# A hybrid decoder layer on one core: the emitter's estimate also books the splits of the weights

## The chip, the cores and the metric

The kernel runs on one core of a Trainium2 chip. The metric is the device time of one execution in microseconds (us), lower is better.

## The reference

One decoder layer over 2048 tokens of width 1024, all in float32. Both branches read the same normed input through one combined projection.

```python
h = rms_norm(x, attn_norm)
proj = h @ w_in                       # gated delta-net q/k/v, z, beta, a; attention q/k/v; two gates
dn_qkv, dn_z, dn_b, dn_a, sq, sk, sv, gate_raw = split_combined(proj)
y_dn  = gated_deltanet_branch(dn_qkv, dn_z, dn_b, dn_a, ...)   # 4 heads of 128, conv of 4, chunks
y_swa = sliding_window_branch(sq, sk, sv, ...)                 # 8 heads of 64, window 128, bias, sinks
gates = sigmoid(gate_raw)
merged = gates[0] * (y_dn @ w_branch_dn) + gates[1] * (y_swa @ w_branch_swa)
x = x + merged @ w_out
h2 = rms_norm(x, ffn_norm)
x = x + (silu(h2 @ w_gate) * (h2 @ w_up)) @ w_down             # inner width 2816
```

## The kernel before

The 2048 tokens are worked in four blocks of 512 (0 to 3). The large matrix products of a block are the dense work. Each float32 operand is split in a high and a low part in a format that TensorE multiplies in one pass, and a product is three matmuls: high by high, high by low, low by high (`mm3`, `tok_mm`). The weights come in 120 units, 118 of 128 by 1024 and two of 128 by 1056 (`skv`). A unit of 1024 serves 24 matmuls of 512 columns, and one dense step is three matmuls.

A unit is fetched by `weights` (lines 154 to 183), which is called right ahead of the unit's first matmul. In block 0 it loads the raw unit (`wraw`, 2 buffers), and for each half ACT copies the high part (line 168) and DVE or POOL subtracts for the low part (line 171; both halves on POOL for the first three units, then the first half on DVE and the second on POOL). Both parts lie in one tile `whl` (5 buffers). Each half is also stored in DRAM. Blocks 1 to 3 load the stored halves straight into `whl` (line 181) and split nothing.

The dense work of a block runs in this order: `skv` and `sq` (keys, values and queries of the attention), the mixer (per delta-net head three `dn` units, one `z` unit; 16 gate units; 4 units of the attention branch; 4 units of the delta-net merge), `wo`, then the feed-forward part in five pieces of `up` and `down`. Block b+1's `skv` and `sq` stand between `wo` and `up` of block b.

All else on TensorE comes from side programs (`norm1`, `norm2`, `skv_post`, `swa`, `dn_post`, two lanes of `dn_cores`, and others): generators that hand out a few instructions on TensorE, DVE, ACT and POOL and then yield until those are done. TensorE's order is fixed by the order of emission (`manual_schedule`), the other engines' order is made by the scheduler, with a higher priority for side programs.

Where a side step goes is settled by `Estimate`. `note` (lines 72 to 94) books each instruction that is emitted through the wrapper `Noted`: it starts when TensorE's own estimated clock `now`, the engine's `free` time and the `ready` times of its inputs plus HOP (220 ns) have passed, and takes a time that grows with its columns. A TensorE instruction moves `now` to its end. What an instruction writes becomes `ready` at its end, by the name of the tile. A side is due when what its step gave out is done, plus HOP and SLACK (30 ns), line 241. `drive` (208 to 228) emits a side step as soon as one is due by `now` and a PSUM bank is free by the estimate, and a dense step otherwise. When dense work waits for a side, sides are emitted until it can go on. `weights` alone takes the unwrapped object, `self.raw`, so that its ACT, DVE and POOL instructions are not booked. Loads are never booked (line 105).

Of the kernel before, what the change touches and what calls it, by code (L numbers as in the profile page):

```python
# [114 lines left out]
class Emitter:  # L115
# [36 lines left out]


    def weights(self, key, a):
        nc = self.raw
        n = a * 264 if key[0] == "skv" else 1024
        h = a // 2
        hl = []
        if key not in self.kept:
            src = self.w_skv[key[1]] if key[0] == "skv" else self.w_all[UNITS[key]]  # L160
            raw = self.wp.tile([P, 1056], F32, name="wraw", tag="wraw", bufs=WR)
            nc.sync.dma_start(out=raw[:, :n], in_=src)
            keep = []
            for j in range(2):
                t = self.wp.tile([P, 2, 528], F32R, name="whl", tag="whl", bufs=WB)
                r = raw[:, j * n // 2:(j + 1) * n // 2]
                hi, lo = t[:, 0, :n // 2], t[:, 1, :n // 2]
                nc.scalar.activation(hi, r, AF.Copy)  # L168
                self.nsub += 1
                eng = nc.vector if self.nsub > 6 and self.nsub % PSUB else nc.gpsimd  # L170
                eng.tensor_tensor(out=lo, in0=r, in1=hi, op=ALU.subtract)  # L171
                if self.nblocks > 1:
                    d = self.kp.tile([P, 2, n // 2], F32, name="wk", tag="wk%d_%d" % (len(self.kept), j))
                    nc.sync.dma_start(out=d, in_=t[:, :, :n // 2].bitcast(F32))
                    keep.append(d)
                hl.append([t[:, e, :n // 2].rearrange("p (a m) -> p a m", a=h) for e in range(2)])
            self.kept[key] = keep
        else:
            for j in range(2):
                t = self.wp.tile([P, 2, 528], F32R, name="whl", tag="whl", bufs=WB)  # L180
                nc.sync.dma_start(out=t[:, :, :n // 2].bitcast(F32), in_=self.kept[key][j])
                hl.append([t[:, e, :n // 2].rearrange("p (a m) -> p a m", a=h) for e in range(2)])
        return lambda k: (hl[k // h][0][:, k % h], hl[k // h][1][:, k % h])
# [914 lines left out]
```

## Time and profile before

| | |
|---|---|
| median of 3 runs | 3195.55 us (3194.09 to 3197.91) |
| profiled execution | 3196.13 us, span 3194.3 us |
| PE (matmul) busy | 3095.3 us, 97% |
| PEld (weight load) busy | 2523.6 us, 79% |
| DVE busy | 1403.2 us, 44% |
| ACT busy | 837.6 us, 26% |
| POOL busy | 415.8 us, 13% |
| mean granted TensorE clock | 0.990 |
| moved by DMA | 595.99 MB |

All times come from one profiled execution. A line of the view in order of time merges neighbouring instructions of one kind: start, length, engine, source line, operation, what it writes and reads, count, and in brackets how long the engine sat idle before it and what ended that. Nearly all instructions carry line 109, that of the wrapper, so they are told apart by the names of their tiles: `kn` and `qr` are normed keys and queries of the attention, `xn` the normed input of the feed-forward part, `R` and `W` belong to the triangular solve of a delta-net head, `O` is a head's output.

### The profile page before, as it was taken

Reading aid. Unit: us, or ns where it says so; the run is one execution under the profiler, and the core shown is the slowest. Engines: PE = TensorE matmul, PEld = TensorE weight load, DVE = VectorE, ACT = ScalarE, POOL = GpSimd, SP = SyncE. Lnnn points to the kernel's source line nnn. Section 1 sums busy time; section 2 is a strip of 40 time slices with the busy share of each in tenths; the row PEclk is TensorE's granted clock in tenths of the full one; section 3 lists DMA queues with packets and bytes.
Section 4 is the critical chain, followed back from the end, with each engine's and each line's share of the span. In section 5 each row is a group of like instructions: output and inputs, shape, how many; then the busy total and the mean of one; then the engine's idle time right before and its main releaser. Section 6 shows DMA issues by size and latency. Waiting matters only on the chain. (4 is left out here: it accounts for less than half of the span.)

```text
span 3194.3 us, 39761 instructions
## 1 busy us (share of the span) xinstructions
PE 3095.3 (97%) x14854; PEld 2523.6 (79%) x14854; DVE 1403.2 (44%) x3626; ACT 837.6 (26%) x2112; POOL 415.8 (13%) x401
## 2 busy tenths in 40 slices
PE   7888989999999999999999999999999999999999
PEld 5776778778888887878887888877888888878887
DVE  5867656533336544542215565443221655422221
ACT  4454334422323322330002323232000233110000
POOL 2433211322212100010001110011000211000000
PEclk9999999999999999999999999999999999999999
DMA  6554475588874446445556445545566544645565
GB/s 240 185 178 152 154 251 209 198 284 285 283 254 145 132 142 215 153 152 191 184 192 200 131 143 179 177 154 170 190 189 205 169 131 133 198 159 193 192 189 183
DMA packets 291848, 595.99 MB, mean 187 GB/s; under 512 B 18975, under 2 KB 20168, under 8 KB 291656
## 3 DMA queue, kind: packets, MB, share of 16 engines
q1 hardware_dynamic: 277648, 569.20, 54.1%
q10 hardware_dynamic: 14008, 24.25, 2.2%
q8 instruction: 117, 1.92, 0.2%
q14 instruction: 75, 0.61, 0.1%
HBM read 459.08 MB, written 134.30 MB: 186 GB/s over the span
## 5 line engine op out<-in xcount | busy, mean ns | idle before, releaser
L109 PE MATMUL acc<-h,whl 128*128 128x512 f32 x7296 | 1760.1, 397 | 7.5 <-DVE whl L171 4.9
L109 PEld LDWEIGHTS acc<-h,whl 128*128 128x128 f32 x7296 | 1357.6, 189 | 313.9 <-DVE whl L171 5.8
L109 PE MATMUL acc<-whl,a 128*128 128x512 f32 x2112 | 493.7, 393 | 0.0
L109 PEld LDWEIGHTS acc<-whl,a 128*128 128x128 f32 x2112 | 395.5, 188 | 90.3
L109 DVE TENSOR_TENSOR x<-x,acc 128x512 f32<-128x512 f32 x192 | 131.4, 687 | 390.4 <-PE acc L109 388.6
L171 POOL TENSOR_TENSOR whl<-wraw,whl 128x512 fp32r<-128x512 f32 (+1 forms) x123 | 167.0, 1359 | 565.4 <-ACT whl L168 472.6
L168 ACT ACTIVATE whl<-wraw 128x512 fp32r<-128x512 f32 (+1 forms) x240 | 149.0, 630 | 290.3 <-PE acc L109 136.1
L109 DVE TENSOR_TENSOR th<-th,acc 128x512 f32<-128x512 f32 x88 | 60.4, 687 | 316.0 <-PE acc L109 315.8
L109 DVE SCALAR_TENSOR_TENSOR th<-th,acc 128x512 f32<-128x512 f32 x88 | 60.5, 687 | 304.9 <-ACT th L109 304.9
L109 PE MATMUL acc<-whl,mt 128*128 128x512 f32 x768 | 181.9, 398 | 8.1 <-DVE h L109 7.6
L109 ACT ACTIVATE th<-acc 128x512 f32<-128x512 f32 x88 | 52.7, 598 | 499.5 <-PE acc L109 499.3
L109 PEld LDWEIGHTS acc<-whl,mt 128*128 128x128 f32 x768 | 145.9, 191 | 43.2 <-DVE h L109 8.5
L109 DVE SCALAR_TENSOR_TENSOR cv<-xr,cst_sb,cv 128x512 f32<-128x512 f32 x144 | 134.6, 935 | 60.7 <-ACT cv L109 53.1
L109 ACT ACTIVATE a<-th 128x512 fp32r<-128x512 f32 x88 | 55.5, 631 | 346.8 <-DVE th L109 332.1
L171 DVE TENSOR_TENSOR whl<-wraw,whl 128x512 fp32r<-128x512 f32 x117 | 89.8, 768 | 121.4 <-ACT whl L168 120.9
L109 PE MATMUL acc<-whl,h 128*128 128x264 f32 (+1 forms) x768 | 139.8, 341 | 0.0
L109 PEld LDWEIGHTS acc<-whl,h 128*128 128x128 f32 x768 | 118.0, 188 | 16.7 <-issue 1.1
L109 POOL COPY ccar<-xr 128x3 f32<-128x3 f32 x48 | 9.0, 188 | 858.5 <-ACT xr L109 858.5
L109 PE MATMUL acc<-sp,whl 128*128 128x512 f32 x384 | 103.2, 409 | 0.0
L109 POOL TENSOR_TENSOR pT<-pT,cst_sb 128x512 f32<-128x512 f32 x62 | 82.7, 1362 | 137.2 <-ACT pT L109 121.1
L109 ACT ACTIVATE L<-L,ast 128x256 f32<-128x256 f32 (+1 forms) x192 | 83.4, 457 | 60.0 <-DVE ast L109 60.0
L109 PE MATMUL acc<-ydn,whl 128*128 128x512 f32 x384 | 92.6, 401 | 0.4
(183 smaller groups left out, 2817.5 us busy)
## 6 DMA issues: line engine op xcount, KB each, us to landing
whl<-wk SPq DMA_DIRECT2D x708, 512.0 KB, 3.9
wk<-whl SPq DMA_DIRECT2D x236, 512.0 KB, 3.5
wraw<-in_w_all SPq DMA_DIRECT2D x118, 512.0 KB, 5.0
x<-in_x ACTq DMA_DIRECT2D x56, 256.0 KB, 5.1
out<-x ACTq DMA_DIRECT2D x32, 256.0 KB, 3.8
whl<-wk SPq DMA_DIRECT2D x12, 528.0 KB, 5.1
wk<-whl SPq DMA_DIRECT2D x4, 528.0 KB, 2.7
x<-in_x SPq DMA_DIRECT2D x8, 256.0 KB, 6.5
```

Of the source, the lines that this page charges most:

```text
L109: r = f(*args, **kw)
L168: nc.scalar.activation(hi, r, AF.Copy)
L171: eng.tensor_tensor(out=lo, in0=r, in1=hi, op=ALU.subtract)
```

## The change

The function `weights` takes the wrapped object. Its ACT copies and its DVE and POOL subtractions are then booked by `Estimate.note` like every other instruction, in their place in the emission; its DMAs are handed on as before. The instructions themselves stay the same.

```diff
     def weights(self, key, a):
-        nc = self.raw
+        nc = self.nc
         n = a * 264 if key[0] == "skv" else 1024
         h = a // 2
         hl = []
```

## Rows read from the trace of the kernel before

**Rows 1.** The page's engine totals: busy us, share of the span, instructions.

```profile
PE 3095.3 (97%) x14854; PEld 2523.6 (79%) x14854; DVE 1403.2 (44%) x3626; ACT 837.6 (26%) x2112; POOL 415.8 (13%) x401
```

**Rows 2.** Busy by stretch: us, PE, PEld, DVE, ACT, POOL, granted clock, DMA share, GB/s.

```profile
100.00:200.00 100.00, 88.73 (x412) 70.54 (x410) 82.79 (x222) 44.41 (x122) 46.78 (x40) 0.95 0.50 174
...
69.00:320.00 251.00, 223.19 (x1120) 178.90 (x1119) 185.52 (x504) 118.43 (x340) 92.64 (x84) 0.95 0.51 176
320.00:412.00 92.00, 79.27 (x437) 65.69 (x436) 56.67 (x145) 33.17 (x79) 20.74 (x15) 0.93 0.52 178
412.00:487.00 75.00, 72.41 (x322) 58.50 (x321) 39.78 (x71) 29.17 (x62) 14.36 (x10) 0.98 0.69 241
487.00:528.00 41.00, 40.06 (x241) 34.95 (x240) 23.86 (x86) 16.19 (x40) 1.28 (x1) 1.00 0.54 190
528.00:645.00 117.00, 111.49 (x526) 86.11 (x525) 70.06 (x209) 58.21 (x157) 44.07 (x37) 0.99 0.60 206
645.00:927.00 282.00, 282.00 (x1221) 228.90 (x1220) 89.55 (x131) 80.34 (x131) 63.63 (x49) 1.00 0.82 285
927.00:3195.00 2268.00, 2240.57 (x10754) 1832.50 (x10752) 900.75 (x2348) 471.62 (x1240) 164.37 (x185) 1.00 0.53 172
```

**Rows 3.** The tile whl, its splits: count, ns min/median/max, first and last start.

```profile
L168 ACT ACTIVATE whl<-wraw x240: 612/632/690, 13.1 to 915.6; 128x512 fp32r<-128x512 f32 x118, 128x528 fp32r<-128x528 f32 x2
L171 POOL TENSOR_TENSOR whl<-wraw,whl x123: 1262/1301/2055, 13.8 to 916.3; 128x512 fp32r<-128x512 f32 x119, 128x528 fp32r<-128x528 f32 x4
L171 DVE TENSOR_TENSOR whl<-wraw,whl x117: 673/692/1778, 34.9 to 913.8; 128x512 fp32r<-128x512 f32 x117
```

**Rows 4.** PE's waits over the span: us in total, times, longest.

```profile
PE acc L109 <- DVE whl L171: 4.9, 2, 3.1
```

**Rows 5.** PE in order of time: first steps of side programs, and dense work.

```profile
51.36 1.30 PE L109 MATMUL aux<-cst_sb,kn 128*128 128x128 f32 x8 [0.77 <-DVE kn L109]
...
430.02 2.19 PE L109 MATMUL aux<-cst_sb,x 128*128 128x128 f32 x12
...
502.81 2.34 PE L109 MATMUL aux<-cst_sb,xn 128*128 128x128 f32 x20
...
527.97 14.04 PE L109 MATMUL acc<-h,whl 128*128 128x512 f32 x60
541.85 0.60 PE L109 MATMUL aux<-cst_sb,qr 128*128 128x128 f32 x4
```

**Rows 6.** ACT and DVE in order of time: the chains ahead of those steps.

```profile
40.93 0.18 ACT L109 ACTIVATE ba<-acc 128x8 f32<-128x8 f32 x1 [0.55 <-PE acc L109]
...
429.28 3.26 DVE L109 TENSOR_SCALAR x<-x,st 128x512 f32<-128x512 f32 x8
...
487.83 0.69 DVE L109 TENSOR_TENSOR x<-x,acc 128x512 f32<-128x512 f32 x1 [0.69 <-PE acc L109]
491.89 3.26 DVE L109 TENSOR_SCALAR xn<-x,st 128x512 f32<-128x512 f32 x8
499.55 0.18 ACT L109 ACTIVATE ba<-acc 128x8 f32<-128x8 f32 x1 [0.38 <-PE acc L109]
503.86 1.42 DVE L109 TENSOR_TENSOR kn<-kr,kst 128x256 f32<-128x256 f32 x4
535.05 2.50 DVE L109 TENSOR_TENSOR qr<-qr,qst 128x512 f32<-128x512 f32 x4
```

**Rows 7.** PE's matmuls on weights (tile whl) in one stretch: us, busy, clock, DMA.

```profile
69.00:320.00 251.00, 166.36 (x658) 0.95 0.51 176
```

**Rows 8.** ACT and PE in order of time, around two waits of PE.

```profile
361.92 0.63 ACT L168 ACTIVATE whl<-wraw 128x512 fp32r<-128x512 f32 x1 [5.13 <-DMA wraw<-in_w_all]
362.46 0.58 ACT L109 ACTIVATE W<-aux 128x512 f32<-128x512 f32 x1
363.09 2.08 PE L109 MATMUL aux<-R,W 128*128 128x128 f32 x8 [4.32 <-ACT W L109]
...
411.65 1.12 PE L109 MATMUL aux<-cst_sb,O 128*128 128x128 f32 x4 [5.77 <-DVE O L109]
```

## The prediction

> **What bounds the kernel now.** I read the engine totals first: PE is busy 97% of the span [rows 1]. With so full an engine the question is where the other 99 us lie, so next came the busy time by stage [rows 2]. The reader is to see three things in it. From 927 us on (blocks 1 to 3) PE is busy 2240.57 of 2268 us, so all three leave 27 us idle. From 645 to 927 us PE is busy 282 of 282, at the full clock, although this stretch splits weights all the time and has no side steps. The rest is in block 0: from 69 to 645 us PE idles 27.8 + 12.7 + 2.6 + 0.9 + 5.5 = 49.5 us, and in four of these five stretches the granted clock is below full, 0.93 to 0.99. So PE's dense stream is the bound, splits alone cost it nothing, and what is lost is lost where side steps lie between matmuls. Then the splits themselves: 240 on ACT of 632 ns, 123 on POOL of 1301 ns, 117 on DVE of 692 ns, all before 918 us [rows 3]. The line of the waits that names most of PE's waits for a split has 4.9 us in 2 waits [rows 4]: the splits run ahead of PE.
>
> **What the change does to the order.** No instruction is added or removed. The estimate now books each split, and it books what a split writes. I worked its rules out by hand from lines 77 to 88. A split of 512 columns takes 160 + 512/1.4 = 526 ns on ACT, the subtraction 70 + 512/0.96 = 603 ns on DVE or 100 + 512 x 2.2 = 1226 ns on POOL, with HOP = 220 ns behind each. They are booked from the moment `weights` is called, which is right ahead of the unit's first matmul. That matmul reads the tile, so its start moves to 526 + 220 + 603 + 220 = 1569 ns after PE's clock in the estimate (2192 ns on POOL), and `est.now` goes with it. Before, a unit of 24 matmuls took 24 x 512/2.4 = 5.12 us there. It will take 6.7 us. If ACT or DVE still has side work booked, the split stands behind that, and the jump is longer by the backlog. At each unit boundary of block 0 the estimated PE thus waits until ACT and DVE have worked off what the sides gave them. Every side that waits for those results is then due, and goes out one dense step (3 matmuls) into the unit.
>
> On the chip that wait doesn't exist [rows 4], and a matmul takes 282/1221 = 0.231 us [rows 2] against 0.213 in the estimate, so a unit is 5.5 us. The estimate was 8% fast for dense work and becomes some 20% slow or more. Side steps move to an earlier place in PE's fixed order, with fewer matmuls between a step and what it reads. Weights that are loaded again (blocks 1 to 3) have no split, nothing is booked, and the state at the start of block 1 has no side left over. I cost 927 to 3194 us at nothing.
>
> **The sum, against the profiled run of 3196.13 us** (span 3194.3; 0.6 above the median of 3195.55).
>
> (a) First steps behind a long chain. Their cover goes down to one dense step, 0.7 us. The ends are zero (the cover stays) and the whole chain less 0.7. `skv_post` of block 0: last accumulation read at 40.93, keys ready when PE's wait ends at 51.36: up to 9 beyond the 0.77 waited now; I take 6, since ACT sat on other issues in that chain. `skv_post` of block 1: 499.55 to 505.28, up to 5; 3. `norm2`: last add ends 488.52, the first half of xn about 493.5, up to 4; 3. `norm1` of block 1: PE leaves the transposes of O at 412.8, so the first merge unit would end at 412.8 + 5.5 = 418.3; PE now takes the first tile at 430.0, up to 11; 4, because DVE does merges in between, which a waiting PE wouldn't send. The queries of block 1: 527.97 to 537.55, up to 9; 5 [rows 5, 6]. Sum 21, from 0 to 38.
>
> (b) The mixer up to 320 us, with both first heads, attention and 12 `dn_post`. PE is busy 223.2 of 251, of which 166.4 is matmuls on weights [rows 2, 7], so 57 is side work. 166.4 is 27 units at about 6.2 us (clock 0.95). With jumps, boundary by boundary, I expect these sides to be out after some 15 units: PE work 57 + 15 x 6.2 = 150 us. DVE's work for them is 185.5 less 12 units' splits at 0.7 = 177 us. The busiest 100 us show DVE at 83% [rows 2]; at that share 177 us take 213, and PE idles 63 against 28. At 95% it is 186 and 36; at today's 74%, 239 and 89. So +8, +35, +61 for full compression; I take 25, since sides also wait for projections that come in dense order, and keep 2 to 60. The 12 units follow later without side work.
>
> (c) 320 to 412 us, heads 2 and 3. PE waits 5.77 us for O at the very end, when the dense work before the merges has run out, and 4.32 for W [rows 8]. Sides that finish earlier save the first; shorter cover for two heads costs about as much. 0, from -12 to +12.
>
> (d) Attention tiles of block 1, to 645 us: PE already idles 5.5 us there, so the cover is just short. Four tiles with 4 boundaries of 1.57 us each lose up to 25; part is slack. I take 6, from 0 to 20.
>
> (e) Clock. In 69 to 412 us, idle 40 us went with a granted clock of 0.95 and 0.93, that is 19 us of work lost. More idle brings more of it, but where PE waits for DVE a slow matmul is partly hidden: 5, from 0 to 25. The Trainium skill ("TensorE: Matmul & The Clock Gate", Part 1) says the throttled state is the default and activity releases it; by that alone I would put this term near its upper end and the sum at about 3270. The rows agree in direction (1.00 where PE never idles).
>
> Sum: 21 + 25 + 0 + 6 + 5 = 57 us. 3196.1 + 57 - 0.6 = **3252 us**.
>
> **The rivals.** *Faster: the load counts, the jump doesn't.* Up to 361.92 us ACT sits idle 5.13 us ahead of a split whose load is late; W of a head stands behind it, and PE waits 4.32 us [rows 8]. If the booked splits mainly push the sides' due times back, PE gets more dense work ahead of such steps. The place is the mixer, the price the 40.5 us idle of 69 to 412 us and its 19 us of clock; if 40% comes back, 3196 - 24 = 3172. It decides if side results come later in the estimate by more than PE's own jump. The Trainium skill (same page, "Architectural detail", queue depths) has ACT and DVE as strict FIFOs, which speaks for this rival: a split at the head does hold what follows. The trace agrees for that one W. Against it: the jump moves PE past the very splits that are booked, so at the first dense step after it ACT and DVE stand free again in the estimate.
>
> *No change.* The cover has slack: xn is complete at 495.15 and PE takes it at 502.81, 7.7 us later [rows 5, 6]. If nearly all steps have so much, the shift only eats slack: 3196, within 6. Against it: PE waits in every stretch with sides.
>
> *Much slower.* The sides get packed so tightly that PE follows DVE's latency through the mixer, at today's 74%: (a) 30, (b) 55, (c) 5, (d) 10, (e) 15 give 3311.
>
> *The change doesn't do what it says.* If the tile read by the matmul had another name than the one booked, PE would not jump and only engine time would count: that ends as the first rival. Both go through the same tile `t`, so I give it nothing of its own.
>
> **How the numbers follow.** Forecast (20 to 90 us slower) 0.61; much slower 0.14; no change 0.10; faster 0.15. About 0.2% is what a measurement here can tell from no change, 6.4 us. The forecast's own range is 3215 to 3286. For 8 in 10 I leave out most of the faster case and the top of the much slower one: 3190 to 3312. Faster 0.15, same 0.10, slower 0.75.
>
> **What would show it.** Right: 927 us to the end keeps its 2268 us; PE's idle time in the first 645 us of work grows by some 50 us, in waits named for DVE (kn, xn, qr, be, R, L) and not for whl; heads 0 and 1 and the attention of block 0 are through PE after some 15 units of that part and not 27; the wait for O is gone; the DVE share of the mixer's first part rises above 0.74. Step (b) is wrong if 27 units still lie in that part; step (a) if kn, xn and qr come as late as now. The whole is wrong if side steps sit later in PE's order than before, or if blocks 1 to 3 change.

## The result: 4.1% slower, and the profile after

| | before | after |
|---|---|---|
| median, us | 3195.79 | 3325.67 |
| ratio (95% interval) | | 1.0409 (1.0396 to 1.0421) |
| span of the profiled execution, us | 3194.3 | 3323.5 |
| PE busy, us | 3095.3 | 3131.3 |
| PE idle (span less busy), us | 99.0 | 192.2 |
| mean granted TensorE clock | 0.990 | 0.973 |

The direction was forecast, the size was not: 3252 was predicted, and 3325.67 lies above the range (3190 to 3312). The 129 us are 93 us more idle time of PE and 36 us by which the same 14854 matmuls got longer. The engine totals of the changed kernel, beside [rows 1]:

```profile
PE 3131.3 (94%) x14854; PEld 2549.6 (77%) x14854; DVE 1387.8 (42%) x3626; ACT 844.0 (25%) x2112; POOL 406.8 (12%) x401
```

Busy time by stretch of the changed kernel, columns as in [rows 2]. They are cut at the same points of the program: the first matmuls of the mixer, the end of heads 0 and 1, the first merge, `skv` of block 1, `up` of block 0, the end of the attention's side steps (748 us; 645 before), the start of block 1 (1056; 927 before). As the side steps end earlier in the dense work, the stretch after them holds more matmuls (1333 against 1221).

```profile
28.00:73.00 45.00, 41.27 (x208) 33.41 (x208) 16.52 (x62) 15.68 (x35) 9.17 (x11) 0.92 0.55 195
73.00:318.00 245.00, 168.01 (x818) 131.64 (x817) 149.48 (x444) 97.63 (x285) 68.93 (x66) 0.84 0.30 104
...
318.00:504.00 186.00, 158.15 (x742) 128.68 (x741) 80.54 (x206) 59.47 (x136) 36.98 (x33) 0.90 0.50 173
...
504.00:589.00 85.00, 75.78 (x339) 62.15 (x338) 42.08 (x73) 31.94 (x68) 14.13 (x11) 0.94 0.74 262
589.00:630.00 41.00, 38.44 (x226) 32.98 (x224) 24.32 (x86) 16.09 (x35) 2.56 (x2) 1.00 0.50 173
630.00:748.00 118.00, 92.75 (x406) 70.69 (x407) 57.69 (x194) 49.97 (x140) 34.42 (x31) 0.86 0.40 134
748.00:1056.00 308.00, 308.00 (x1333) 250.10 (x1333) 97.25 (x143) 87.93 (x144) 70.38 (x54) 1.00 0.83 286
1056.00:3324.00 2268.00, 2241.41 (x10757) 1833.29 (x10755) 901.13 (x2349) 471.46 (x1240) 164.47 (x185) 1.00 0.53 172
```

Blocks 1 to 3 take 2268 us in both, with 26.6 us idle after and 27.4 before. All of the loss is in block 0, and it goes with side steps: where none are left (748 to 1056), PE is never idle. By the starts of the same work in both traces, the first matmuls of the mixer come 4.8 us later (68.85 to 73.62), the first merge 92.3 (412.42 to 504.7), `wo` 102.5 (440.4 to 542.9), `skv` of block 1 and `up` of block 0 both 99.6 (for `up`, 527.97 to 627.53), the last split 129.7 (916.3 to 1046.0), and the end 129.2.

What PE waits for up to 1060 us in the changed kernel (us in total, times, longest):

```profile
PE aux L109 <- DVE cv L109: 44.9, 11, 6.4
PE aux L109 <- DVE x L109: 29.7, 5, 11.4
PE aux L109 <- POOL be L109: 21.2, 4, 9.0
PE aux L109 <- DVE R L109: 18.0, 4, 10.5
PE aux L109 <- ACT L L109: 16.1, 4, 5.0
PE aux L109 <- DVE qr L109: 12.1, 2, 6.1
```

All six are first reads of a side's result (`cv` is what `dn_post` makes of one projection of a head, `be` a step ahead of the triangular solve, `L` the attention's scores), and no wait for a split is left; [rows 4] had two. About 20 us of the wait for x are the start of the kernel, as before. PE in order of time, at some of these steps, beside [rows 5, 8]:

```profile
48.22 1.94 PE L109 MATMUL aux<-cst_sb,kn 128*128 128x128 f32 x8 [3.17 <-DVE kn L109]
...
73.62 0.85 PE L109 MATMUL acc<-h,whl 128*128 128x512 f32 x3
...
80.61 1.09 PE L109 MATMUL aux<-cst_sb,qr 128*128 128x128 f32 x4 [6.14 <-DVE qr L109]
...
113.84 5.80 PE L109 MATMUL acc<-h,whl 128*128 128x512 f32 x24
...
127.92 1.12 PE L109 MATMUL aux<-cst_sb,cv 128*128 128x128 f32 x4 [5.24 <-DVE cv L109]
...
168.34 1.11 PE L109 MATMUL aux<-cst_sb,R 128*128 128x128 f32 x4 [10.54 <-DVE R L109]
...
471.49 0.66 PE L109 MATMUL aux<-cst_sb,O 128*128 128x128 f32 x4 [0.59 <-DVE O L109]
525.85 6.79 PE L109 MATMUL aux<-cst_sb,x 128*128 128x128 f32 x32 [9.22 <-DVE x L109]
...
602.39 2.34 PE L109 MATMUL aux<-cst_sb,xn 128*128 128x128 f32 x20
...
627.53 0.85 PE L109 MATMUL acc<-h,whl 128*128 128x512 f32 x3
634.36 1.09 PE L109 MATMUL aux<-cst_sb,qr 128*128 128x128 f32 x4 [5.97 <-DVE qr L109]
```

The kernel before, at the first of these steps:

```profile
68.85 14.05 PE L109 MATMUL acc<-h,whl 128*128 128x512 f32 x60
82.75 0.60 PE L109 MATMUL aux<-cst_sb,qr 128*128 128x128 f32 x4
83.10 3.70 PE L109 MATMUL acc<-h,whl 128*128 128x512 f32 x15
86.64 0.60 PE L109 MATMUL aux<-cst_sb,cv 128*128 128x128 f32 x4
```

The queries show the mechanism as drawn. In the kernel before, 60 matmuls of the next units stood ahead of their transposes (68.85 in block 0; 527.97 in block 1 [rows 5]); now it is one dense step of 3 (73.62; 627.53), and PE waits 6.14 and 5.97 us. The posts (`cv`) went the same way. Before, 75 matmuls of the mixer stood ahead of the first post's transposes (86.64), 24 of them its own unit, so 51 were cover. Now 24 matmuls lie between one post and the next (113.84): the last 21 of the unit and 3 of the one behind it, which are all the cover. The wait for O at the mixer's end fell from 5.77 to 0.59 us. The transposes of xn stand where they stood.

### The profile page after: what moved, and what is told of

The parts are those of the page before. It is cut to its first block, busy times and chain, and to the rows that moved or that the text cites. A ratio compares the mean times of both kernels' runs of the same rounds, so it can differ in the third digit from the quotient of the medians.

```text
span 3323.5 us, 39753 instructions
## 1 busy us (share of the span) xinstructions
PE 3131.3 (94%) x14854; PEld 2549.6 (77%) x14854; DVE 1387.8 (42%) x3626; ACT 844.0 (25%) x2112; POOL 406.8 (12%) x401
## 5 line engine op out<-in xcount | busy, mean ns | idle before, releaser
L109 PE MATMUL acc<-h,whl 128*128 128x512 f32 x7296 | 1798.1, 402 | 0.0
L109 PEld LDWEIGHTS acc<-h,whl 128*128 128x128 f32 x7296 | 1374.1, 192 | 305.9 <-issue 1.6
L109 DVE SCALAR_TENSOR_TENSOR cv<-xr,cst_sb,cv 128x512 f32<-128x512 f32 x144 | 127.0, 882 | 69.9 <-ACT cv L109 67.3
```

The source lines that it names most:

```text
L109: r = f(*args, **kw)
```

## Experiments

The theory: the loss comes from TensorE's own estimated clock, which at each unit that is split jumps to the end of all booked side work. The rivals: the load on the engines' free times, the bare wait for a split, and loss that is only handed on.

### Jump without load, and load without jump

In the first, the engines' free times are put back after a unit's splits are booked:

```diff
+            free = dict(self.est.free)
             for j in range(2):
                 ...
+            self.est.free = free
             self.kept[key] = keep
```

> The splits are booked as in the changed kernel, and TensorE's estimated clock waits for them, but afterwards the engines' free times are set back, so that side steps are not charged for the splits. Jump theory (the loss comes from TensorE's estimated clock moving ahead at each unit): as slow as the changed kernel, 3310 to 3340 us, PE idle about 190 us. Load theory (the loss comes from the engine time of the splits in the estimate): close to the kernel before, 3190 to 3230 us.

Measured: 3326.20 us, 1.0421 (1.0406 to 1.0437), PE idle 192.8 us. Its trace has the very order of instructions of the changed kernel on TensorE, ACT, DVE and POOL: once the clock jumps, the load adds nothing.

In the second, `weights` takes the unwrapped object again and only charges the engines:

```diff
+                est = self.est
+                for e, ns in (("scalar", 526), ("vector", 603) if eng is nc.vector else ("gpsimd", 1226)):
+                    est.free[e] = max(est.free.get(e, 0.0), est.now) + ns
```

> The engine time of each split is added to ACT's and to DVE's or POOL's free time in the estimate (526, 603 or 1226 ns), but what the split writes is not booked, so TensorE's estimated clock does not jump. Jump theory: side steps only get later, so no loss: 3165 to 3205 us, and PE's idle time in block 0 stays at or below 99 us in all. Load theory: most of the loss is here, above 3270 us.

Measured: 3206.15 us, 1.0042 (1.0027 to 1.0057), just above the range that the jump theory gave, and PE idles 102.6 us, where it gave at most 99: a small loss, no gain. PE in order of time at the end of its mixer:

```profile
406.03 1.09 PE L109 MATMUL aux<-cst_sb,O 128*128 128x128 f32 x4 [5.29 <-DVE st L109]
...
431.60 1.08 PE L109 MATMUL aux<-cst_sb,O 128*128 128x128 f32 x4 [4.66 <-DVE O L109]
```

Between these two PE waits eight times more, six of them for results of the last head: the sides got later, as the faster rival wanted, and the dense work ran out before them. So that rival falls: its mechanism moves the loss to the end of the mixer.

### The fixed step, and the backlog alone

Moving the estimated clock by the price of one split on idle engines, and nothing else:

```diff
             keep = []
+            self.est.now += 1569
             for j in range(2):
```

> No split is booked; TensorE's estimated clock is moved by 1569 ns at each unit that is split, which is the jump with idle engines. If the bare wait for a split is what costs, most of the loss appears: 3280 us or more. If it is the backlog of side work ahead of the split, by which the jump grows, a third or less: 3215 to 3245 us.

Measured: 3211.23 us, 1.0063 (1.0046 to 1.0080). This is 18 us, about a seventh of the loss and a little below the range given.

Moving it only up to the end of the side work booked on ACT and DVE, with no price for the split:

```diff
             keep = []
+            est = self.est
+            est.now = max(est.now, est.free.get("scalar", 0.0), est.free.get("vector", 0.0))
             for j in range(2):
```

> No split is booked; at each unit that is split, TensorE's estimated clock is only moved up to the time at which the estimate has ACT and DVE done with all side work given out so far. Backlog theory: this alone makes nearly the whole loss of the changed kernel, 3285 to 3330 us, since the fixed step of 1569 ns alone gave 3211. If backlog and the split's own time are both needed for the loss (each below what the other covers): 3200 to 3260 us.

Measured: 3322.89 us, 1.0409 (1.0393 to 1.0425), the ratio of the changed kernel, with 46.0 us in 11 waits for cv. The backlog is the cause: at each unit the estimate makes PE wait for the sides' own work, though the dense matmuls don't read it. The order of work on ACT, DVE and POOL changes in block 0 together with TensorE's, and no run holds one fixed while the other moves.

### Where the parts of the loss lie

Only the mixer's units booked:

```diff
-        nc = self.nc
+        nc = self.nc if key[0] in ("dn", "g", "br") else self.raw
```

> The changed kernel, but only the units of the mixer (heads, gates, branches) are booked. By the two traces the mixer up to the merges is 88 us longer, the first merges 10, attention in the feed-forward part 29, the start 4. If these parts add up: 3195 + 88 + 10 = 3293, 3280 to 3305 us. If the loss of one part is only handed on to the next: within 10 us of the changed kernel, or below 3260 us.

Measured: 3291.51 us, 1.0309 (1.0295 to 1.0323). The parts add up: 3.1 of the 4.1% belong to the mixer and its hand-over to the merges, the other 1.0% to the units outside it.

The changed kernel with dn_post held back:

```diff
         yield
+        if len(self.kept) < 120:
+            yield 5000
         ps = self.aux()
```

> The changed kernel, but in block 0 dn_post yields 5000 ns of estimated time more before its transposes, so that they have dense work ahead of them. In the changed kernel PE waits 45 us in 11 waits for them (DVE cv), and the matmuls behind run at the lower clock. If those waits are a loss of their own: 35 to 65 us less, 3260 to 3290 us. If the heads wait for the posts anyway and the idle time only goes to the next step of the heads (be, R): 3310 to 3330 us.

Measured: 3293.86 us, 1.0319 (1.0305 to 1.0333), 32 us less than the changed kernel (29 by the ratios), and 4 us above the end of the range for a loss of its own. What PE waits for up to 1060 us there:

```profile
PE aux L109 <- ACT L L109: 25.6, 5, 9.5
PE aux L109 <- DVE L L109: 15.2, 5, 5.2
...
PE aux L109 <- DVE O L109: 12.5, 3, 8.7
...
PE aux L109 <- DVE cv L109: 0.7, 1, 0.7
```

The wait for cv went from 44.9 to 0.7 us, but those for L rose from 25.4 (16.1 on ACT, 9.3 on DVE) to 40.8 and that for O from 2.6 to 12.5 us. In sum PE's idle time fell by 25.6 us (192.2 to 166.6) and its busy time by 6.4. So the waits for the posts, the largest single wait, were a loss of their own, but over 40% of what they gave up was handed on to other steps.

### Later sides in the kernel before

> The kernel before, with 1000 ns more ahead of each side step that waits for results, as long as weights are still being split (block 0). Jump theory, read backwards: with more matmuls ahead of each side step PE waits less in block 0; 3165 to 3185 us. Rival: the side programs then end later than the dense work of the mixer, and PE waits longer for O at its end; 3195 to 3230 us.

```diff
-... ) + HOP + SLACK
+... ) + HOP + SLACK + (1000 if len(self.kept) < 120 else 0)
```

Measured: 3197.85 us, 1.0016 (1.0007 to 1.0026). No gain; in block 0 PE waits 7.8 us for O in place of 5.8, and 11.3 for kd in place of 5.3. The rival holds here: 1000 ns more of cover on every step isn't what the kernel before lacks.

### What does hold PE in the kernel before

[rows 8] show W behind a split whose load is late. Three raw weight buffers let loads run further ahead; one side buffer had to go for the space.

```diff
-NU = 63
-WR = 2
+NU = 62
+WR = 3
```

> The kernel before with three raw weight buffers instead of two (and one side buffer fewer, for the space); TensorE's order of instructions is the same. In the kernel before some side results stand behind a split whose load is late (W behind 5.13 us, vb, T). If late loads hold them: PE's idle time in block 0 falls by 5 to 20 us, 3170 to 3190 us. If the splits wait for something else: 3190 to 3198 us.

Measured: 3183.41 us, 0.9973 (0.9963 to 0.9983): faster than both kernels. The control, with the side buffer gone and two raw buffers:

> The kernel before with one side buffer fewer (62 instead of 63) and the two raw weight buffers it had; TensorE's order is the same. It parts the two edits of the kernel with three raw buffers. If the third raw buffer is what gained there: 3188 to 3198 us, no change. If the side buffer did it: 3180 to 3187 us.

Measured: 3191.45 us, 0.9989 (0.9980 to 0.9998). By the ratios, 0.11% of the gain of 0.27% came with the side buffer, at the edge of what can be measured, and some 0.16%, 5 us, with the third raw buffer (the two intervals just overlap). PE's waits of the kernel with three raw buffers, up to 1060 us, beside [rows 4, 8]:

```profile
PE aux L109 <- DVE O L109: 5.8, 1, 5.8
PE aux L109 <- ACT T L109: 5.5, 1, 5.5
...
PE acc L109 <- DVE whl L171: 1.8, 1, 1.8
...
PE aux L109 <- ACT W L109: 0.9, 1, 0.9
```

The wait for a split on DVE fell from 4.9 to 1.8 us, and stays 4.9 in the control. The wait for W fell from 4.32 to 0.9, but to 0.9 in the control as well, so W isn't what the third buffer frees. In the kernel before, the late load of [rows 8] is issued at 355.61 us, after ACT took a split of an earlier unit at 352.57, behind a side copy (`sp`) that had waited 5.47 us for DVE. In the control that copy doesn't wait, the split runs at 346.95 and the load is issued at 349.62. So the late load did hold W, but the control frees it with two buffers. The wait for T grew by 2 us (5.5; 3.48 before), and which waits make up the 5 us isn't shown. The Trainium skill ("TensorE: Matmul & The Clock Gate", "Architectural detail") calls ACT and DVE strict FIFOs; the trace agrees for W, which starts right behind the split that waits for its load [rows 8] and comes without that wait where the load is earlier, with the same order on TensorE.

The third raw buffer and 300 ns more ahead of side steps in block 0:

> Three raw buffers, and 300 ns more ahead of each side step in block 0. With 1000 ns more and two raw buffers, the loss at the end of the mixer (O) ate the gain. If a smaller delay pays before that end takes it back: 3170 to 3181 us. If waits of single steps are set by other things than their cover: 3181 to 3190 us.

Measured: 3195.63 us, 1.0002 (0.9994 to 1.0011), outside both ranges: the delay took the whole gain back. PE waits 8.8 us for O there and 7.9 for T.

### The estimate's rate of TensorE

```diff
-            end = start + max(n / 2.4 * ...
+            end = start + max(n / 2.2 * ...
```

> The kernel before, with TensorE's rate in the estimate set to what the trace shows (2.2 columns per ns in place of 2.4, 0.231 us for 512 columns), in all four blocks. All side steps come about 8% earlier in dense work. If each step has little slack, PE's waits grow in all blocks: 3205 to 3240 us. If slack covers it: within 8 us of the kernel before.

Measured: 3221.80 us, 1.0084 (1.0070 to 1.0098). Blocks 1 to 3, which start at 929 us:

```profile
929.00:3222.00 2293.00, 2250.34 (x10756) 1836.66 (x10754) 906.35 (x2349) 469.40 (x1240) 157.04 (x185) 0.99 0.53 170
```

They take 2293 us against 2268 in the kernel before, and PE idles 43 us there against 27. Block 0 takes 929 us against 927, with no more idle time than before (71.5 and 72.3). The true rate makes the kernel slower: the 8% by which the estimate is fast for dense work are cover that the side steps of blocks 1 to 3 live on. Block 0, where they were expected to count too, hardly changes.

### The clock

The same matmuls take 36 us longer at the lower granted clock. Is that a cost of its own? The changed kernel with work of no use ahead of dn_post's transposes, into the PSUM bank that they overwrite, first 40 matmuls of 128 columns, then 9 of 512 (the diff is the second):

```diff
         ps = self.aux()
+        if len(self.kept) < 120:
+            for _ in range(9):
+                self.raw.tensor.matmul(ps, self.slr, self.kv.kth[0], start=True, stop=True)
```

> The changed kernel, with 40 matmuls of 128 columns ahead of each dn_post's transposes in block 0, into the PSUM bank that the transposes then overwrite: work of no use, in the place where PE waits 45 us for cv. If the lower clock after idle time is a cost of its own: the matmuls on weights in the mixer get shorter, and the time falls by 4 to 20 us, 3305 to 3322 us. If PE is held by the sides and not by its clock there: no gain, 3323 to 3335 us.

Measured: 3345.43 us, 1.0472 (1.0458 to 1.0486). A group of 40 took 4.57 to 8.78 us, and the twelve together more than they took off the wait for cv (44.9 to 14.9 us); PE's busy time grew by 53 us and the granted clock of 73 to 318 us was 0.83. This tells nothing of the clock, as the fill was too large.

> The changed kernel with 9 matmuls of 512 columns (2.1 us at the full clock) ahead of each dn_post's transposes in block 0, into the PSUM bank that the transposes overwrite: work of no use, less than half of what the 40 short matmuls took. PE waits 45 us in 11 waits for cv there, so most of this fits into idle time. If the lower clock is a cost that goes with idle time and comes back with work: the granted clock of the mixer's first part rises from 0.84 to above 0.88 and the time falls by 3 to 15 us, 3310 to 3322 us. If PE is held by the sides there whatever its clock: 3322 to 3335 us.

Measured: 3325.53 us, 1.0408 (1.0391 to 1.0426), the time of the changed kernel. Its stretches in the mixer:

```profile
73.00:318.00 245.00, 183.80 (x896) 143.45 (x895) 153.18 (x444) 97.14 (x285) 68.90 (x66) 0.87 0.31 105
318.00:504.00 186.00, 164.19 (x770) 133.69 (x769) 80.70 (x207) 60.44 (x138) 35.86 (x33) 0.91 0.49 171
```

108 more matmuls cost nothing: PE's idle time fell by 21.5 us and its busy time rose by 22.0. The granted clock rose from 0.84 to 0.87 (the mean of time at 1.2 and at 2.4 GHz), and the largest group of matmuls on weights got 6 us shorter (1798.1 to 1792.1), but no time came back: so far as the clock rose, PE is held by the sides there. The Trainium skill ("TensorE: Matmul & The Clock Gate", Part 1) says that activity releases the throttle; the granted clock agrees, the time doesn't follow. The clock stayed below the 0.88 that the expectation had asked for, so how much a fully granted clock would give stays open.

## Why the prediction was wrong, point by point

*What bounds the kernel, and what the change does to the order*: right. The loss lies in block 0 alone, in waits for first reads of side results (93 us more idle time) and in the longer matmuls that go with them (36); the runs with the jump alone, the load alone and the backlog alone show that the jump of TensorE's estimated clock makes it. The text had the jump as 1569 ns plus the backlog. The backlog is nearly all of it: 4.09% alone, against 0.63% for the fixed step alone.

*(a), first steps behind long chains*: the list was wrong in both directions. The start cost 4.8 us (6 taken) and the queries of block 1 5.97 (5 taken). `norm1` cost 10 us by the starts of merges and `wo` (4 taken, 11 as the end). These three come to the 21 us taken for all five, by luck: `norm2` and the second `skv_post` cost nothing (6 taken). Their dense cover, `skv` and `sq` of block 1, are units that block 0 has split already, so nothing is booked and the order stays. And the twelve `dn_post` were in no term with a chain of their own. They are the same case as the queries, a chain on ACT and DVE behind a unit with the next unit's jump ahead of its result, and they are the largest wait of the changed kernel: 44.9 us in 11. I had put them under DVE's load in (b).

*(b), the mixer's first part*: this is the step that failed most. Its part on the order held, its part on the bound fell. Counted in the two traces, the output of head 1 leaves PE after 15.2 units of the mixer (26.8 before), as the 15 I took. But I priced it by DVE's share and expected more than 0.74. It fell to 149.48 of 245 us, 0.61, and PE's idle time was 77 us there, above the 63 that I had for full compression. The share is a mean over two states. In PE's 14 waits of over 2 us in this stretch DVE is busy 57.12 of 67.68 us, 0.84; in the rest of it, 0.52. These are the longest of them, for R, and the sum of all 14, columns as in [rows 2]:

```profile
157.80:168.34 10.54, 0.01 (x1) 0.00 (x0) 9.75 (x27) 1.55 (x3) 5.05 (x5) 0.58 0.13 50
...
sum 67.68, PE 0.05 PEld 0.14 DVE 57.12 ACT 18.95 POOL 32.47; mean PE 0.00 PEld 0.01 DVE 4.08 ACT 1.35 POOL 2.32
```

So PE and DVE work in turn. PE waits for single chains (be, R, cv), mostly on DVE and for be on POOL, and while PE works DVE is half idle. My sum had DVE near full all through the stretch, with PE's work beside it. A bound from an engine's share is a lower bound for idle time, not an estimate.

*(c), heads 2 and 3*: the wait for O went as said, 5.77 to 0.59. What the shorter cover costs was mis-sized: PE idles 27.9 us from 318 to 504 us (12.7 from 320 to 412 before), of it 14.9 for cv of head 3, 7.2 for R and 5.1 for be. Together, the way from the first mixer unit to the first merge grew by 87.5 us, where (b) and (c) had 25 and the posts nothing.

*(d), attention tiles of block 1*: from `up` to the last split 30.1 us more, of which 6 belong to the queries; 24 against 6 taken and 20 as the end. Each tile lost about 5 us at L (4.11, 4.98, 4.99 in the last three): I had counted boundaries at 1.57 us each, without the backlog that the tile itself makes.

*(e), the clock*: 36 us of longer matmuls against 5 taken and 25 as the end. The lengths of stretches named under (a) to (d) hold their share of these 36 already. The clock fell to 0.84 and 0.90 in the mixer and to 0.86 in the tiles. By the short fill this isn't, in the mixer, a cost that simply adds to the idle time.

*The rivals*: "faster" falls by the run with the load alone, and "no change" by the result. "Much slower", 3311, had the right mechanism with DVE's latency, at a chance of 0.14, and was 15 us short. The slack that spoke for "no change" (xn taken 7.7 us late) belongs to a step that the change doesn't move.

## What to carry to other kernels

When an emitter places work by its own clock, a booking that makes that clock wait moves all that follows, not only what it books: ask what the waited-for instruction is queued behind in the model, and if the chip queues it there too. Here the splits run ahead on the chip and stand behind the side work in the model. A better-informed estimate is no better placement by itself: the true matmul rate cost 0.8%, since the old error had been cover of the side steps, and the true engine load 0.4%, since with it the sides ended later than the dense work ahead of the merges. And price a step that loses its cover by the latency of its own chain, for each chain that is spawned there; an engine's busy share over a stretch only says how little the loss can be, as it mixes PE's waits with the rest.

## What was not expected of the hardware

A matmul that reloads its weights for 128 columns took about 0.115 us (40 in 4.58 us) where 512 columns take 0.231 us: twice the time per column. And 108 matmuls of 512 columns in PE's waits raised the granted clock from 0.84 to 0.87 without any effect on the time. In the wait for R (157.80 to 168.34 us), four instructions of DVE in a row on 36 to 44 columns took 1.18 to 1.31 us each, where their neighbours took 0.20, and they lie in the 4.92 us in which POOL works on four tiles `pT`. In the whole trace 7 of the 480 instructions of this kind took over 0.6 us, and all 7 overlap with work of POOL; no run tests the cause.
